# Row norm factors moved from GpSimd to VectorE, and a shorter inverse root, in a transformer block on one core

## The chip, the core and the metric

The kernel runs on one core of a Trainium2 chip. The core has TensorE (PE, matrix products), VectorE (DVE), ScalarE (ACT), GpSimd (POOL) and SyncE (SP, which issues most of the DMAs). The metric is the device time of one execution in microseconds, lower is better; the time given is the median of several runs.

## The reference

One block: two RMS norms with modulation, a mixer of four gated linear-attention heads (HGRN2) and four retention heads, run forwards and backwards over 2048 rows of width 1024, then a feed-forward part with a convolution of width 3 on its gate, and a final RMS norm. A context of 256 rows supplies the start states. What matters here are the norms: each row is multiplied with the inverse root of its mean square.

```python
def _rmsnorm(t, g):
    tf = t.astype(jnp.float32)
    y = tf * lax.rsqrt(jnp.mean(tf * tf, axis=-1, keepdims=True) + EPS)
    return (y * g.astype(jnp.float32)).astype(t.dtype)

hx = _rmsnorm(x, norm1_g[layer]) * (1.0 + sc1) + sh1
hc = _rmsnorm(ctx, norm1_g[layer]) * (1.0 + csc1) + csh1
...
hg_o = _rmsnorm(hg_o, hg_norm_g.reshape(HG_HEADS, 1, HG_DV))
ret_o = _rmsnorm(y_f + _flip(y_b), ret_norm_g.reshape(RET_HEADS, 1, RET_DV))
x = x + g1 * (mix_x.astype(x.dtype) @ w_out[layer])
hx2 = _rmsnorm(x, norm2_g[layer]) * (1.0 + sc2) + sh2
x = x + g2 * _conv_ffn(hx2, w_up[layer], conv_w[layer], conv_b[layer], w_down[layer])
return _rmsnorm(x, final_g)
```

## The kernel before, in words

The 2048 rows are four groups of 512; each group is four tiles of 128 rows on the partitions. Products in f16 are made of three passes each (`mm3`, L99 to L104: high times high, high times low, low times high), and the large matrices are multiplied in seven block products, whose sums and differences VectorE, ScalarE and, for the feed-forward weights, GpSimd form.

The program runs in this order. `setup` and `heads` (L1063) load the modulation weights and normalise group 3, the first one that is used. Then the eight heads are worked off in 32 steps, each with a group's sweep (the tiles K, Q, T and A, the products `sc`, `sf`, `kp`, `op`) woven together with the next step's projection (`hx` or `hc` times `w_z`, `w_q`, `w_vg`). Into the first of these steps the norms of the remaining rows are laid: group 2 and the context (called `gate` in the trace, after the tiles in which its rows lie) while the first projection runs, group 1 during step 0 and group 0 during step 1. After the heads come the output projection (`out_steps`, L1484), the feed-forward part and `ffn_down` (L1850), which ends with the final norm, row tile by row tile.

`norm_rows` (L395) does one group's norm: squares with row sums on ScalarE (and, for group 2, group 3 and the context, half of them on VectorE), their sum `ssq` on VectorE (L413), the inverse root by `rstd` (L414), and the scaling of the rows in place, half of each row on ScalarE (L419) and half on VectorE (L421). `first_blocks` (L431) then transposes the scaled rows on TensorE (`tp`, L428), applies the modulation on ScalarE (`ftmp`, L471) and forms the seven feature blocks `hx` (`hc` for the context).

There are two ways to the inverse root. `rstd` (L68) uses six operations on GpSimd: scale and add, a power of -0.5, and one Newton step. `rstd_v` (L80) uses twelve on VectorE: scale and add, a start value from the bits of the number in two operations, and three Newton steps of three operations. Both write the same small tiles `rs_v`, `rs_t` (one buffer) and `rs_y` (two buffers). `rstd` is called for the five norms in `norm_rows` and the 16 row tiles of `out_steps`; `rstd_v` for the 32 head norms (L997) and for the 16 row tiles of the final norm (L1912).

The order of the instructions on each engine is made by a scheduler from the program's dependences, its own estimates of durations, and hints in the code (`issue_after`, `high_priority`). Each engine then works its list off in order. So a few operations more or less on one engine change the places of many others.

Of the kernel before, what the change touches and what calls it, by code (L numbers as in the profile page):

```python
# [12 lines left out]
I32 = mybir.dt.int32  # L13
U8 = mybir.dt.uint8
AF = mybir.ActivationFunctionType
ALU = mybir.AluOpType
# [4 lines left out]
D = 1024  # L21
KT = D // P
G = 512
NG = SEQ // G
# [18 lines left out]
H = G // 2  # L43
RING = 10
SEQUENCE = 0, 1, 5, 6, 4, 3, 2

# [7 lines left out]
class Kern:  # L56
# [23 lines left out]
    def rstd_v(self, ssq, n, count):  # L80

        tt, ts, stt = self.nc.vector.tensor_tensor, self.nc.vector.tensor_scalar, self.nc.vector.scalar_tensor_tensor
        v, y, t = (self.wp.tile([P, 4], F32, tag=f"rs_{a}", bufs=1 + (a == "y"), name="rs_" + a)[:, :n] for a in "vyt")
        ts(v, ssq, 1.0 / count, EPS, ALU.mult, ALU.add)
        ts(t.bitcast(I32), v.bitcast(I32), 1, None, ALU.logical_shift_right)
        ts(y.bitcast(I32), t.bitcast(I32), -1, 0x5F3759DF, ALU.mult, ALU.add)
        for _ in range(3):
            stt(t, y, -0.5, y, ALU.mult, ALU.mult)
            tt(t, t, v, ALU.mult)
            stt(y, t, 1.5, y, ALU.add, ALU.mult)  # L90
        return y

    def ps(self, tag, shape, name):
# [301 lines left out]
    def norm_rows(self, g, xn, behind=None, both=False, late=None):  # L395

        nc = self.nc
        nt = len(xn)
        if g == NG - 1:
            self.junk = self.mp.tile([P, 512], F16, tag="qf3", bufs=1, name="junk")  # L400
        if both:
            junk = self.mp.tile([P, 512], F16, tag="Ta", bufs=1, name="junk")
        sq = self.mp.tile([P, 4, 2], F32, tag="sq8", bufs=2, name="sq8")
        for i in range(nt):
            for h in range(2):
                on_act = not both or h
                with self.tc.issue_after(behind[on_act].ins) if behind else nullcontext():
                    if on_act:
                        nc.scalar.activation(self.junk, xn[i][h], AF.Square, accum_out=sq[:, i, h:h + 1])
                    else:  # L410
                        nc.vector.scalar_tensor_tensor(junk, xn[i][h], 1.0, xn[i][h], ALU.mult, ALU.mult, accum_out=sq[:, i, h:h + 1])
        ssq = self.mp.tile([P, 4], F32, tag="ssq", bufs=2, name="ssq")
        nc.vector.tensor_tensor(ssq[:, :nt], sq[:, :nt, 0], sq[:, :nt, 1], ALU.add)  # L413
        r = self.rstd(self.mp, ssq[:, :nt], nt, D)  # L414
        for i in range(nt):
            for h in range(2):
                if h:
                    with self.tc.issue_after(late.ins) if late else nullcontext():
                        nc.scalar.activation(xn[i][h], xn[i][h], AF.Copy, scale=r[:, i:i + 1])  # L419
                else:  # L420
                    nc.vector.tensor_scalar(xn[i][h], xn[i][h], r[:, i:i + 1], None, ALU.mult)  # L421
        return xn
# [126 lines left out]

    def features(self, h, g, ms=SEQUENCE):  # L550

        if g in self.X:
            return self.X.pop(g)
        X = [None] * 7
        for m in ms:
            X[m] = self.slot_tile([P, 4, 2, H], F16, "hx", "hx")
            self.nc.sync.dma_start(X[m], self.hxd[g][m])
        return X
# [1473 lines left out]
```

## Time and profile before

| what | value |
|---|---|
| median of 3 runs | 2556.37 us (2556.28 to 2559.72) |
| the profiled execution | 2557.44 us, its span 2555.7 us |
| granted TensorE clock, mean | 0.990 |
| GpSimd busy | 386.9 us, nearly all of it in the feed-forward part |
| first and last GpSimd operation for `norm_rows` | 28.4 us, 147.9 us |
| operations of `rstd` and `rstd_v` | 21 calls on GpSimd, 48 calls on VectorE |

The page gives busy times by engine. Shares of the whole span say little here, since the kernel has stages with different limits; the busy times of stretches, and what each engine waited for in them, say more. A row of the timeline has start, duration, engine, line, operation, the tile written and those read, sizes and count, and in brackets the engine's idle time before it and what ended it.

### The profile page before, as it was taken

The numbers are of one execution on the slowest core, as the hardware profiler recorded it, in microseconds if no ns is written. First come the engines' busy times: TensorE is split into PE (matmuls) and PEld (weight loads), VectorE is DVE, ScalarE is ACT, GpSimd is POOL, SyncE is SP. The second block draws the span as 40 slices with busy tenths as digits, with TensorE's granted clock in tenths as the row PEclk, the third lists the DMA queues.
The fourth block names the chain that finished last, engine by engine and source line by source line (L and its number), as shares of the span: only waits on it lengthen the run. The fifth ranks groups of instructions, "written<-read, shape, count | busy, mean of one in ns | idle before, by whom it ended". The sixth has DMA issues, their size and how long they took to land.

```text
span 2555.7 us, 56261 instructions
## 1 busy us (share of the span) xinstructions
PE 2476.7 (97%) x22763; PEld 1644.6 (64%) x22763; DVE 1892.4 (74%) x4309; ACT 1354.8 (53%) x2886; POOL 386.9 (15%) x377
## 2 busy tenths in 40 slices
PE   6899999999999999999999999999999999999998
PEld 4688989898899999985454444444444444444443
DVE  6888787878677877875658888887888887224756
ACT  7786666656545544554556565555665555211221
POOL 1100000000000000001230343434343443000000
PEclk8899999999999999999999999999999999999999
DMA  8415243334466767785320233322333338534562
GB/s 313 169 63 193 90 159 131 115 124 142 162 207 211 265 213 247 254 313 194 106 78 30 85 114 120 108 107 99 110 113 104 108 130 301 205 142 157 216 221 78
DMA packets 144788, 402.36 MB, mean 157 GB/s; under 512 B 16143, under 2 KB 16371, under 8 KB 139920
## 3 DMA queue, kind: packets, MB, share of 16 engines
q1 hardware_dynamic: 134976, 381.81, 42.7%
q10 hardware_dynamic: 9248, 16.79, 2.0%
q8 instruction: 178, 2.92, 0.5%
q14 instruction: 82, 0.67, 0.1%
q0 software_dynamic: 304, 0.17, 0.0%
HBM read 302.77 MB, written 95.94 MB: 156 GB/s over the span
## 4 chain that ended last, share of the span: by engine, by line
PE 66%; DVE 16%; issue 6%; ACT 5%; DMA 5%; POOL 1%; SPq 0%; DVEq 0%; ACTq 0%; POOLq 0%
PE pa L102 7%; PE pa L103 7%; PE pa L104 7%; PE pd L104 5%; PE pd L102 5%; PE pd L103 5%; PE pc L102 3%; PE pc L104 3%; PE pc L103 3%; PE pb L102 2%; PE pb L103 2%; PE pb L104 2%; PE opp L103 2%; PE opp L104 2%; PE opp L102 2%
## 5 line engine op out<-in xcount | busy, mean ns | idle before, releaser
L104 PE MATMUL pa<-feat,w 128*128 128x512 f16 x704 | 266.6, 379 | 1.9 <-DVE w L704 1.9
L102 PE MATMUL pa<-feat,w 128*128 128x512 f16 x704 | 263.6, 379 | 4.6 <-ACT ta L596 4.5
L103 PE MATMUL pa<-feat,w 128*128 128x512 f16 x704 | 266.8, 379 | 0.0
L103 PE MATMUL pd<-wd,actl 128*128 128x512 f16 x616 | 233.3, 379 | 0.0
L104 PE MATMUL pd<-wd,actl 128*128 128x512 f16 x616 | 233.3, 379 | 0.0
L102 PE MATMUL pd<-wd,actl 128*128 128x512 f16 x616 | 232.6, 379 | 0.0
L104 PEld LDWEIGHTS <-w 128*128 128x128 f16 x1232 | 120.5, 98 | 147.5 <-DVE w L704 2.6
L103 PEld LDWEIGHTS <-w 128*128 128x128 f16 x1232 | 120.5, 98 | 144.9 <-issue 5.3
L102 PEld LDWEIGHTS <-w 128*128 128x128 f16 x1232 | 120.4, 98 | 142.1 <-ACT w L703 1.3
L103 PEld LDWEIGHTS <-hx 128*128 128x128 f16 x1824 | 179.4, 98 | 8.3 <-issue 6.4
L102 PEld LDWEIGHTS <-hx 128*128 128x128 f16 x1824 | 179.6, 99 | 1.8 <-ACT hx L447 0.2
L104 PEld LDWEIGHTS <-hx 128*128 128x128 f16 x1824 | 179.0, 98 | 1.4 <-DVE hx L448 0.7
L1507 POOL TENSOR_TENSOR ssq<-ssq 128x1 f32<-128x1 f32 x16 | 7.0, 439 | 1111.4 <-ACT junk L1502 1111.4
L1752 ACT ACTIVATE st<-act,modT 128x512 f16<-128x512 f32 x154 | 107.3, 717 | 114.8 <-DVE act L1742 64.9
L102 PE MATMUL pa<-w_vg,hx 128*128 128x128 f16 x896 | 160.6, 220 | 3.0 <-ACT ct L596 1.4
L104 PE MATMUL pa<-w_vg,hx 128*128 128x128 f16 x896 | 160.4, 220 | 0.5 <-DVE hx L448 0.5
L1753 DVE SCALAR_TENSOR_TENSOR st<-act,modT,st 128x512 f16<-128x512 f32 x154 | 142.6, 961 | 24.5 <-ACT st L1752 23.9
L103 PE MATMUL pa<-w_vg,hx 128*128 128x128 f16 x896 | 160.7, 220 | 0.0
L102 PE MATMUL pa<-hx,w_z 128*128 128x256 f16 x512 | 140.9, 275 | 6.4 <-ACT ct L596 4.1
L104 PE MATMUL pa<-hx,w_z 128*128 128x256 f16 x512 | 140.8, 275 | 1.9 <-issue 1.9
L103 PE MATMUL pa<-hx,w_z 128*128 128x256 f16 x512 | 140.9, 275 | 0.5 <-DVE hx L451 0.4
L102 PE MATMUL pc<-feat,w 128*128 128x512 f16 x352 | 133.4, 379 | 0.8 <-ACT w L703 0.8
(545 smaller groups left out, 7219.0 us busy)
## 6 DMA issues: line engine op xcount, KB each, us to landing
hx<-hxd SPq DMA_DIRECT2D x212, 512.0 KB, 5.0
actd<-st SPq DMA_DIRECT2D x154, 256.0 KB, 2.0
actl<-actd SPq DMA_DIRECT2D x28, 1024.0 KB, 5.2
wur<-in_w_up_dram SPq DMA_DIRECT2D x44, 512.0 KB, 3.6
raw<-in_w_in_dram SPq DMA_DIRECT2D x36, 512.0 KB, 4.7
wm<-in_w_mod_dram SPq DMA_DIRECT2D x64, 256.0 KB, 4.2
hxd<-hx SPq DMA_DIRECT2D x28, 512.0 KB, 3.6
wdb<-in_w_down_dram SPq DMA_DIRECT2D x44, 256.0 KB, 4.1
```

The lines of the kernel that those rows point to most:

```text
L102: mm(ps, lhs(0), rhs(0), start=start, stop=False, skip_group_check=True)
L103: mm(ps, lhs(0), rhs(1), start=False, stop=False, skip_group_check=True)
L104: mm(ps, lhs(1), rhs(0), start=False, stop=stop, skip_group_check=True)
L1507: nc.gpsimd.tensor_tensor(ssq[:, 0:1], ssq[:, 0:1], ssq[:, 1:2], ALU.add)
L1752: nc.scalar.activation(p[:, 0], v, AF.Copy, scale=s)
L1753: nc.vector.scalar_tensor_tensor(p[:, 1], v, s, p[:, 0], ALU.mult, ALU.subtract)
```

## The change

The row norm factors of every group but group 3 are made by `rstd_v` on VectorE in place of `rstd` on GpSimd; that is group 2, the context, group 1 and group 0. `rstd_v` itself gets nine operations in place of twelve: the start value comes from one operation in place of two, and three Newton steps are replaced by one polynomial of degree four in the deviation `v` of y*y*x from 1, which is evaluated in Horner's way and multiplied on. `rstd` on GpSimd stays for group 3 and for the 16 row tiles of `out_steps`.

```diff
+RSQ = 0.7235660666409525, -0.6910196001212606, 0.7162674493934401, -0.8287177420385489
...
         ts(v, ssq, 1.0 / count, EPS, ALU.mult, ALU.add)
-        ts(t.bitcast(I32), v.bitcast(I32), 1, None, ALU.logical_shift_right)
-        ts(y.bitcast(I32), t.bitcast(I32), -1, 0x5F3759DF, ALU.mult, ALU.add)
-        for _ in range(3):
-            stt(t, y, -0.5, y, ALU.mult, ALU.mult)
-            tt(t, t, v, ALU.mult)
-            stt(y, t, 1.5, y, ALU.add, ALU.mult)
+        ts(y.bitcast(I32), v.bitcast(I32), -0.5, float(0x5F3759DF), ALU.mult, ALU.add)
+        tt(t, y, y, ALU.mult)
+        tt(t, t, v, ALU.mult)
+        ts(v, t, RSQ[0], -RSQ[0], ALU.mult, ALU.add)
+        stt(t, v, RSQ[3], v, ALU.add, ALU.mult)
+        stt(t, t, RSQ[2], v, ALU.add, ALU.mult)
+        stt(t, t, RSQ[1], v, ALU.add, ALU.mult)
+        stt(y, t, 1.0, y, ALU.add, ALU.mult)
         return y
...
-        r = self.rstd(self.mp, ssq[:, :nt], nt, D)
+        r = self.rstd(self.mp, ssq[:, :nt], nt, D) if g == NG - 1 else self.rstd_v(ssq[:, :nt], nt, D)
```

Behind the changed function the line numbers are three higher than before (L421 becomes L424, L930 becomes L933).

The scheduler moves instructions over the first steps. On VectorE in step 0, around group 1's factor (`x` are group 1's rows, `T`, `cFG` and `ct`, `cb` tiles of the sweep and of projections), there stands before:

```order
L451 TENSOR_TENSOR hc_156<-ftmp,hc_156 128x2x128
L791 TENSOR_TENSOR T_1307<-FG 128x512
L421 TENSOR_SCALAR x_1201<-x_1201,rs_y 128x512
L421 TENSOR_SCALAR x_1203<-x_1203,rs_y 128x512
L421 TENSOR_SCALAR x_1205<-x_1205,rs_y 128x512
L421 TENSOR_SCALAR x_1207<-x_1207,rs_y 128x512
L791 TENSOR_TENSOR T_1772<-T_1307 128x256
L630 TENSOR_TENSOR ct<-pc,ct 128x128
L630 TENSOR_TENSOR cb<-pa,cb 128x128
```

and in the changed kernel:

```order
L87 TENSOR_TENSOR rs_t<-rs_y 128x4
L633 TENSOR_TENSOR ct<-pc,ct 128x128
L794 TENSOR_TENSOR T_1781<-T_1316 128x256
L88 TENSOR_TENSOR rs_t<-rs_t,rs_v 128x4
L633 TENSOR_TENSOR cb<-pa,cb 128x128
L89 TENSOR_SCALAR rs_v<-rs_t 128x4
L90 SCALAR_TENSOR_TENSOR rs_t<-rs_v 128x4
L91 SCALAR_TENSOR_TENSOR rs_t<-rs_t,rs_v 128x4
L788 TENSOR_SCALAR cFG<-cFG,omlb,lb 128x256
L92 SCALAR_TENSOR_TENSOR rs_t<-rs_t,rs_v 128x4
L93 SCALAR_TENSOR_TENSOR rs_y<-rs_t,rs_y 128x4
L424 TENSOR_SCALAR x_1207<-x_1207,rs_y 128x512
```

The T product and the two evacuations moved from behind the scaling to the midst of the chain of nine, whose first two operations stand further ahead.

On TensorE the transposes of group 1 (`tp`) stood right behind the context's last products with `w_z`:

```order
L103 MATMUL pa<-hc_157,w_z 128x128
L104 LDWEIGHTS w_z
L104 MATMUL pa<-hc_157,w_z 128x128
L428 MATMUL tp<-ident,x_1201 128x128
L428 MATMUL tp<-ident,x_1202 128x128
```

In the changed kernel 36 products stand between these two, the last of them products of `hx` (group 2's features) with `w_z`:

```order
L106 MATMUL pc<-hx,w_z 128x256
L107 LDWEIGHTS w_z
L107 MATMUL pc<-hx,w_z 128x256
L431 MATMUL tp<-ident,x_1207 128x128
L431 MATMUL tp<-ident,x_1208 128x128
```

Twelve of the 36 are products of the context, 128 columns wide, and 24 are of group 2, 256 wide; all of them stood behind the first twelve transposes before.

On VectorE in step 1, around group 0's factor (`x` are group 0's rows, K, Q and T the tiles of step 0's sweep), there stands before:

```order
L413 TENSOR_TENSOR ssq<-sq_2158 128x4
L791 TENSOR_TENSOR T_1930<-T_1891 128x32
L630 TENSOR_TENSOR ct<-pc,ct 128x256
L925 TENSOR_TENSOR K<-K,T_1891 128x2x16x16
L421 TENSOR_SCALAR x_2142<-x_2142,rs_y 128x512
L421 TENSOR_SCALAR x_2144<-x_2144,rs_y 128x512
L421 TENSOR_SCALAR x_2146<-x_2146,rs_y 128x512
L421 TENSOR_SCALAR x_2148<-x_2148,rs_y 128x512
L930 TENSOR_TENSOR Q<-Q,T_1891 128x2x16x16
```

and in the changed kernel, from the sixth operation of the chain on:

```order
L90 SCALAR_TENSOR_TENSOR rs_t<-rs_v 128x4
L928 TENSOR_TENSOR K<-K,T_1939 128x2x8x32
L933 TENSOR_TENSOR Q<-Q,T_1939 128x2x8x32
L91 SCALAR_TENSOR_TENSOR rs_t<-rs_t,rs_v 128x4
L794 TENSOR_TENSOR T_2275<-FG 128x512
L92 SCALAR_TENSOR_TENSOR rs_t<-rs_t,rs_v 128x4
L928 TENSOR_TENSOR K<-K,T_2275 128x2x128x2
L93 SCALAR_TENSOR_TENSOR rs_y<-rs_t,rs_y 128x4
L424 TENSOR_SCALAR x_2151<-x_2151,rs_y 128x512
L424 TENSOR_SCALAR x_2153<-x_2153,rs_y 128x512
L424 TENSOR_SCALAR x_2155<-x_2155,rs_y 128x512
L424 TENSOR_SCALAR x_2157<-x_2157,rs_y 128x512
```

The K and Q products of the sweep's sixth level (8x32), which the product `sf` of TensorE needs, stood behind the scaling and now stand in front of it; those of the fifth level (16x16) are now ahead of the sum `ssq`. On ScalarE, likewise, most of the copies of A (L940, and four of the six of L937) moved from behind its four scalings of group 0 to in front of them.

## What to expect of it

> **What bounds the kernel now.** I read the page's busy times first, then busy time by stage, then TensorE's waits inside the first 250 us, and last the end of the timeline.
>
> ```profile
> span 2555.7 us, 56261 instructions
> PE 2476.7 (97%) x22763; PEld 1644.6 (64%) x22763; DVE 1892.4 (74%) x4309; ACT 1354.8 (53%) x2886; POOL 386.9 (15%) x377
> 50.00:250.00 200.00, 181.93 (x2834) 161.43 (x2832) 177.03 (x425) 162.43 (x373) 11.92 (x24) 0.95 0.37 135
> 250.00:1200.00 950.00, 926.88 (x13163) 845.71 (x13163) 732.03 (x2014) 528.15 (x1321) 7.57 (x28) 1.00 0.56 187
> 1200.00:2400.00 1200.00, 1190.37 (x5910) 553.47 (x5909) 854.96 (x1489) 606.58 (x1082) 359.42 (x304) 1.00 0.37 128
> 2400.00:2546.40 146.40, 146.36 (x679) 66.13 (x676) 92.78 (x270) 22.01 (x53) 0.00 (x0) 1.00 0.46 165
> ```
>
> TensorE is the bound: it sits idle for 79 us of the span. From 250 us on it is idle for 23.1 us of 950, 9.6 of 1200 and nothing of the last 146, so a VectorE operation saved there is mostly saved beside TensorE. What the change can move is the stretch from 50 to 250 us, with 18.1 us of idle and a mean clock of 0.95, and the tail behind the last product.
>
> The four lines of TensorE's timeline that hold its longest waits near a norm factor, and the stretches of 2 us around them (columns: length, PE, PEld, DVE, ACT, POOL busy, then granted clock):
>
> ```profile
> 104.99 0.58 PE L428 MATMUL tp<-ident,x 128*128 128x128 f32 x3 [1.95 <-DVE x L421]
> 105.74 1.70 PE L428 MATMUL tp<-ident,x 128*128 128x128 f32 x9 [0.18 <-ACT x L419]
> 153.33 0.69 PE L918 MATMUL sf<-Q,K 128*64 128x64 f32 x16 [2.20 <-DVE Q L930]
> 154.85 0.80 PE L964 MATMUL op<-V,A 128*128 128x128 f32 x2 [0.83 <-ACT A L937]
> 106.00:108.00 2.00, 2.00 (x13) 1.36 (x12) 0.76 (x4) 2.00 (x5) 0.00 (x0) 0.67 0.00 0
> 108.00:110.00 2.00, 2.00 (x12) 1.44 (x11) 0.07 (x1) 1.89 (x4) 0.00 (x0) 0.50 0.00 0
> 154.00:156.00 2.00, 1.17 (x35) 0.93 (x38) 1.95 (x4) 0.82 (x4) 0.00 (x0) 0.61 0.00 0
> 156.00:158.00 2.00, 2.00 (x59) 1.94 (x48) 1.39 (x3) 1.53 (x3) 0.00 (x0) 0.50 0.04 8
> 158.00:160.00 2.00, 2.00 (x15) 1.94 (x14) 1.86 (x4) 1.98 (x7) 0.00 (x0) 0.50 0.02 4
> 160.00:162.00 2.00, 2.00 (x59) 1.90 (x59) 1.46 (x5) 2.00 (x6) 0.00 (x0) 0.68 0.00 0
> ```
>
> TensorE waits 2.13 us before group 1's transposes and 3.03 us while group 0's factor is made, and behind each wait it runs some microseconds at a lower clock. The work lost to that, (1 - clock) x busy: 0.66 + 1.00 = 1.7 us near 108, and 0.46 + 1.00 + 1.00 + 0.64 = 3.1 us near 158.
>
> Both waits begin at GpSimd:
>
> ```profile
> 98.76 0.15 DVE L413 TENSOR_TENSOR ssq<-sq 128x4 f32<-128x4 f32 x1
> 98.83 0.28 DVE L630 TENSOR_TENSOR ct<-pb,ct 128x128 f32<-128x128 f32 x1
> 99.00 3.12 POOL L72 TENSOR_SCALAR rs_v<-ssq 128x4 f32<-128x4 f32 x1 [28.55 <-DVE ssq L413]
> 104.12 0.20 POOL L77 TENSOR_TENSOR rs_y<-rs_y,rs_t 128x4 f32<-128x4 f32 x1
> 102.00:104.00 2.00, 1.03 (x19) 0.86 (x16) 0.06 (x1) 0.00 (x0) 1.67 (x5) 1.00 0.00 0
> 104.35 1.67 DVE L421 TENSOR_SCALAR x<-x,rs_y 128x512 f32<-128x512 f32 x4 [2.30 <-POOL rs_y L77]
> 104.35 2.56 ACT L419 ACTIVATE x<-x,rs_y 128x512 f32<-128x512 f32 x4 [2.59 <-POOL rs_y L77]
> 147.95 1.68 DVE L421 TENSOR_SCALAR x<-x,rs_y 128x512 f32<-128x512 f32 x4 [2.02 <-POOL rs_y L77]
> 147.95 2.56 ACT L419 ACTIVATE x<-x,rs_y 128x512 f32<-128x512 f32 x4 [2.77 <-POOL rs_y L77]
> 164.22 0.60 PE L428 MATMUL tp<-ident,x 128*128 128x128 f32 x4
> ```
>
> The factor comes 5.4 us after group 1's sum, and VectorE and ScalarE, which work in order, both stand still before it for 2.0 to 2.8 us. For group 0 nobody needs the scaled rows yet: their first transpose is at 164.22. The stall alone, sitting in front of the K and Q products, costs TensorE its 3.03 us.
>
> **The change, part by part.** Operations off the path first. 48 calls lose three operations each; dependent ones start 0.19 us apart:
>
> ```profile
> 2548.85 0.15 DVE L84 TENSOR_SCALAR rs_v<-cw 128x1 f32<-128x1 f32 x1
> 2550.97 0.16 DVE L90 SCALAR_TENSOR_TENSOR rs_y<-rs_t,rs_y 128x1 f32<-128x1 f32 x1
> 2551.16 1.42 DVE L1915 SCALAR_TENSOR_TENSOR c<-c,rs_y,fgb 128x512 f32<-128x512 f32 x2
> L89 DVE TENSOR_TENSOR rs_t<-rs_t,rs_v x144: 145/160/166, 261.1 to 2550.8; 128x4 f32<-128x4 f32 x96, 128x1 f32<-128x1 f32 x48
> ```
>
> *Tail.* The last call is on the path: 12 operations from 2548.85 to 2551.16, 0.193 each. Nine take 1.73 in place of 2.31: -0.6 us. The new operations are of the same forms and widths (145 to 166 ns), so I see no other price; were each 20 ns longer, 0.2 us would be given back. The 15 other calls of the last norm lie beside a TensorE that is never idle there: 0.
>
> *Head norms.* 32 calls x 3 x 0.19 = 18 us of VectorE time between 250 and 1200 us, where it is busy for 732 of 950. TensorE's idle of 23.1 us there is the most it could return; the other instructions change places too, which could cost as much as a lost load wait, so I bound it by -3 and +3 and take 0.
>
> *Group 1.* The VectorE chain stands between products and evacuations that used to wait behind the scaling. From the sum to the factor the new order holds what VectorE did without a pause from 98.76 to 102.06 (the row of 102 has it busy for 0.06 us), 3.3 us, some 0.8 us of evacuations and T from behind the scaling (an estimate from their widths, by the 0.28 of the evacuation at 98.83), and nine small operations, five of them at 0.07 (98.76 to 98.83: an independent follower starts that soon) and four at 0.19, 1.1 us. That is 5.2 us, about the 5.4 of before: the factor is not sooner. But VectorE does its work in the meantime, and TensorE has 36 products ahead of the transposes, 24 of them of the form below, which start 0.11 us apart: 2.6 us and more, for a wait of 2.13.
>
> ```profile
> 71.99 0.27 PE L102 MATMUL pb<-hx,w_q 128*128 128x256 f16 x1
> 72.10 0.27 PE L103 MATMUL pb<-hx,w_q 128*128 128x256 f16 x1
> ```
>
> So the wait goes and with it the low clock: -2.1 - 1.7 = -3.8; bounds 0 and -3.8.
>
> The Trainium skill, "TensorE: Matmul & The Clock Gate", section "What's actually happening", has the clock halve after an idle window of about 3.4 us. Here 2.13 us of idle in two pieces were followed by 0.50, so the rows speak for a lower limit; by the page's window the gap would not be the cause and the term would be -2.1.
>
> *Group 0.* K and Q products stand ahead of, or inside, the chain, and the four scalings behind. On VectorE's path to the product at 153.33 the stall of 2.02 and the scalings' 1.6 go, and six dependent and three single operations come, 6 x 0.19 + 3 x 0.07 = 1.4: 2.2 us sooner, just the wait of 2.20; besides, K by FG and the K and Q of one level more now stand ahead of the sum, not behind the factor. Most of ScalarE's copies of A move ahead of its scalings (2.77 + 2.46 us sooner), which covers the 0.83. The scaled rows come later but have 164.22 - 149.55 = 14.7 us to spare. So -3.0 - 3.1 = -6.1; bounds 0 and -6.1.
>
> *Group 2 and context.* Here the chain has a price.
>
> ```profile
> 64.92 0.16 DVE L413 TENSOR_TENSOR ssq<-sq 128x4 f32<-128x4 f32 x1
> 68.25 1.68 DVE L421 TENSOR_SCALAR x<-x,rs_y 128x512 f32<-128x512 f32 x4 [1.21 <-POOL rs_y L77]
> 68.44 0.22 PE L104 MATMUL pc<-w_vg,hx 128*128 128x128 f16 x1
> 70.98 0.86 DVE L421 TENSOR_SCALAR gate<-gate,rs_y 128x512 f32<-128x512 f32 x2
> 76.09 0.69 DVE L451 TENSOR_TENSOR hx<-ftmp,hx 128x512 f16<-128x512 f32 x1
> 80.00:90.00 10.00, 6.58 (x103) 4.16 (x102) 10.00 (x21) 10.00 (x25) 0.00 (x0) 0.98 0.86 316
> 90.00:100.00 10.00, 6.24 (x37) 4.55 (x37) 10.00 (x26) 8.96 (x27) 1.00 (x1) 0.51 0.50 203
> ```
>
> FG, cb and ct now stand inside the chain, and ct waits for a product that TensorE ends near 68.7. So group 2's factor comes near 69.6, 1.4 us late, but with FG, cb and ct done. The context's chain waits behind qs, K, Q and ks and ends near 75.8, against 70.98. Adding VectorE's rows up, it is about 0.6 us behind at 76 us, shortly before the stretch from 80 to 100 in which it has no idle time and ScalarE hardly any. I take +0.6; bounds -0.5 and the context's whole delay, +4.8.
>
> *VectorE's load.* The four groups bring 36 operations into a stretch where VectorE is busy for 177 of 200 us. Between independent work each costs 0.07, together +2.5; in a row, 0.19 each, +7.0. I take +2.5, since most stand between other work. It hides in VectorE's idle only if TensorE does not catch up with it, and it will: the terms of groups 1 and 0 take 10 us out of that stretch.
>
> *GpSimd and SyncE.* GpSimd loses 24 operations of 4 calls and nothing waits for it sooner. Some loads and stores of feature blocks and of raw weights change places on SyncE, which issues in order.
>
> ```profile
> ACT w_z L750 <- DMA raw<-in_w_in_dram: 26.8, 11, 4.3
> ```
>
> ScalarE's longest wait for such a load is 4.3 us, the most that one place further back should cost; the order moves some forward and some back, so I take 0, bounds -1 and +4.3.
>
> Sum: -0.6 + 0 - 3.8 - 6.1 + 0.6 + 2.5 = -7.4 us. The profiled execution took 2557.44 us (1.7 around its span), 1.1 above the median of 2556.37. So 2550.0 for it, and **2549.0** for the median.
>
> **Rivals.** (1) *VectorE becomes the bound.* The 36 operations cost 0.19 each and TensorE, come early, waits for K and Q products: -7.4 + (7.0 - 2.5) = -2.9, 2553.5. For it: VectorE is already full from 80 to 100. Against: 2.0 and 2.3 us of its own idle go at the same time. The skill's "VectorE: DVE Perf Modes", section "The DRAIN you can't avoid", holds that an operation starts only when the pipe has emptied, and advises fewer operations whatever their chaining; that is this rival. The pair at 98.76 and 98.83 speaks against it. (2) *Hidden anyway.* The factors come no sooner and something else is late: casts of feature blocks on ScalarE for group 1, sums of squares for group 0. Only the tail stays: 2555.8. (3) *Slower.* The context's factor is made behind FG, which waits for ScalarE's sigmoid, which now stands behind four scalings that wait for group 2's factor. If that circle costs the full 4.8 us at 76, all behind it is late by as much, TensorE's idle grows into a longer low clock (+3.1, as near 158), and groups 1 and 0 give nothing since VectorE is late when they come: +4.8 + 3.1 - 0.6 = +7.3, 2563.7. It decides once VectorE's first cast behind ks starts later than 78 us (76.1 now). (4) *Everything is returned:* no load, no delay: -10.5, 2545.9.
>
> **How the numbers follow.** Forecast 0.55, rival 1 0.15, rival 2 0.14, rival 3 0.08, rival 4 0.08. A measurement can tell 0.2%, 5.1 us: below 2551.3 is faster, above 2561.5 slower. Of the forecast's 0.55 I put 0.05 above 2551.3. Faster 0.50 + 0.08 = 0.58; same 0.05 + 0.15 + 0.14 = 0.34; slower 0.08. The range runs from 2543 (rival 4 and the head norms' -3) to 2558 (rival 2 with +2 from moved instructions).
>
> **What would show it.** Right: no wait of TensorE over 1 us before group 1's transposes and before sf and op of the first head, clock 1.00 there, nine operations of 1.7 us in the tail. Wrong at group 2: the first cast behind ks later than 77 us. Wrong at the load: new waits of TensorE on VectorE's K, Q or hx between 110 and 220 us. Wrong altogether: the tail is shorter and the first 250 us as long as before.

## The result, and the profile after

| | runs | median, us | lowest to highest |
|---|---|---|---|
| before | 6 | 2559.27 | 2556.28 to 2561.57 |
| after | 6 | 2542.45 | 2536.08 to 2547.92 |

The ratio of after to before is 0.9938, with a 95% interval of 0.9926 to 0.9949: the change makes the kernel faster by 0.6%, about 16 us. In the two profiled executions it is 14.8 us (spans 2555.7 and 2540.9). The forecast was -7.4 us, to 2549.0 us within 2543 to 2558: the direction came out, the gain is twice as large, and the median lies half a microsecond below the stated range. Two executions at a much lower clock are left out of all comparisons, one of 7359 us at 0.34 (the variant with one operation more behind the first head norm; of its trace only the order of the instructions is used) and one of 3199 us at 0.75 (the kernel before).

The page of the changed kernel begins as follows, and below it are two of the stretches shown for the kernel before (length, then PE, PEld, DVE, ACT and POOL busy, then the granted clock):

```profile
span 2540.9 us, 56141 instructions
PE 2469.5 (97%) x22763; PEld 1638.8 (64%) x22763; DVE 1880.3 (74%) x4201; ACT 1354.4 (53%) x2886; POOL 373.3 (15%) x353
50.00:250.00 200.00, 184.62 (x2927) 165.49 (x2926) 186.24 (x480) 166.14 (x386) 0.00 (x0) 0.97 0.39 142
250.00:1200.00 950.00, 929.92 (x13147) 843.91 (x13146) 722.10 (x1909) 534.65 (x1328) 10.36 (x35) 1.00 0.56 191
```

TensorE has the same number of products; its busy time falls by 7.3 us, since less of it is run at the low clock, and its idle time by 7.5 (14.8 less 7.3). In the first stretch the clock goes from 0.95 to 0.97 and the idle time from 18.1 to 15.4; in the second the idle time goes from 23.1 to 20.1.

Where along the program the gain arises is read from rows that both kernels have. The first `kp` of the third step (the first row before, the second after), and the end of the last norm, where nine operations are made in a row:

```profile
298.90 1.09 PE L947 MATMUL kp<-ident,K 128*128 128x128 f32 x8
```

```profile
291.01 1.09 PE L950 MATMUL kp<-ident,K 128*128 128x128 f32 x8
2534.64 0.15 DVE L85 TENSOR_SCALAR rs_v<-cw 128x1 f32<-128x1 f32 x1
2536.18 0.16 DVE L93 SCALAR_TENSOR_TENSOR rs_y<-rs_t,rs_y 128x1 f32<-128x1 f32 x1
2536.38 1.41 DVE L1918 SCALAR_TENSOR_TENSOR c<-c,rs_y,fgb 128x512 f32<-128x512 f32 x2
```

So 7.9 of the 14.8 us are there by 300 us. The chain of the tail takes 2536.38 - 2534.64 = 1.74 us in place of 2.31, 0.6 us. What is left, some 6 us, arises between 300 us and the end of the output projection, in the heads; a table further on divides it.

TensorE's waits from 50 to 110 us, and below them those from 110 to 170 us, in the changed kernel (sum, times, longest):

```profile
PE pb L105 <- DVE ct L633: 3.7, 1, 3.7
PE tp L431 <- ACT ftmp L474: 1.7, 4, 0.5
...
PE pa L105 <- ACT ct L599: 2.0, 2, 1.1
```

The wait of `tp` for `x` is gone, and so are those for Q and A. The longest one that is left was there before, 2.7 us long, and has grown by 1.0; two waits for `ct`, 2.0 us together, are new between 110 and 170 us. The stretches around the two places, and group 1's and group 2's rows:

```profile
102.00:104.00 2.00, 1.75 (x29) 1.63 (x29) 2.00 (x8) 1.05 (x4) 0.00 (x0) 1.00 0.00 0
106.00:108.00 2.00, 2.00 (x23) 1.88 (x21) 2.00 (x6) 2.00 (x4) 0.00 (x0) 1.00 0.00 0
150.00:160.00 10.00, 10.00 (x223) 9.62 (x222) 8.29 (x21) 9.42 (x20) 0.00 (x0) 1.00 0.02 4
100.18 0.16 DVE L416 TENSOR_TENSOR ssq<-sq 128x4 f32<-128x4 f32 x1
105.53 0.16 DVE L93 SCALAR_TENSOR_TENSOR rs_y<-rs_t,rs_y 128x4 f32<-128x4 f32 x1
107.34 1.36 PE L431 MATMUL tp<-ident,x 128*128 128x128 f32 x11
69.71 0.88 DVE L424 TENSOR_SCALAR x<-x,rs_y 128x512 f32<-128x512 f32 x2
75.84 0.89 DVE L424 TENSOR_SCALAR gate<-gate,rs_y 128x512 f32<-128x512 f32 x2
77.25 0.68 DVE L454 TENSOR_TENSOR hx<-ftmp,hx 128x512 f16<-128x512 f32 x1
```

The clock is full at both places. Group 1's factor is no quicker than before (105.53 + 0.16 - 100.18 = 5.5 us from the start of the sum; 104.12 + 0.20 - 98.76 = 5.6 before), and its first transposes start later (107.34, before 104.99), but TensorE has other products until then.

### The profile page after: what moved, and what is told of

Same layout as the page of the kernel before. It is cut to its first block, busy times and chain, and to the rows that moved or that the text cites. A ratio compares the mean times of both kernels' runs of the same rounds, so it can differ in the third digit from the quotient of the medians.

```text
span 2540.9 us, 56141 instructions
## 1 busy us (share of the span) xinstructions
PE 2469.5 (97%) x22763; PEld 1638.8 (64%) x22763; DVE 1880.3 (74%) x4201; ACT 1354.4 (53%) x2886; POOL 373.3 (15%) x353
## 4 chain that ended last, share of the span: by engine, by line
PE 74%; DVE 13%; ACT 5%; DMA 4%; issue 3%; POOL 0%; SPq 0%; DVEq 0%; ACTq 0%; POOLq 0%
PE pa L105 8%; PE pa L106 8%; PE pa L107 8%; PE pd L107 5%; PE pd L105 5%; PE pd L106 5%; PE pc L105 4%; PE pc L106 4%; PE pc L107 4%; PE pb L105 3%; PE pb L106 3%; PE pb L107 3%; PE opp L105 2%; PE opp L107 2%; PE opp L106 2%
```

## The experiments

Twelve variants ran. The one idea is that the move took away stalls of VectorE and with them TensorE's waits in the first 300 us; the others concern the 6 us in the heads: the time of the operations saved there, the scheduler's new order, or luck with the low clock. The table gives all results; "idle" is 600 us less TensorE's busy time from 720 to 1320 us of the profile, that is in the second half of the heads and the output projection, and "clock" is the granted clock, mean of all executions that are compared.

| variant | operations in a head norm | row factors on VectorE | median, us | ratio to before, 95% | idle, us | clock |
|---|---|---|---|---|---|---|
| before | 12 | none | 2556.8 to 2559.3 | 1 | 9.9 | 0.991 |
| the change | 9 | 2, context, 1, 0 | 2542.45 | 0.9938 (0.9926 to 0.9949) | 7.1 | 0.993 |
| move alone | 12 | the same, 12 operations | 2551.71 | 0.9979 (0.9967 to 0.9990) | 8.7 | 0.993 |
| polynomial alone | 9 | none | 2551.82 | 0.9973 (0.9960 to 0.9986) | 6.0 | 0.991 |
| change, heads with 12 | 12 | 2, context, 1, 0 | 2560.28 | 1.0001 (0.9993 to 1.0010) | 16.6 | 0.992 |
| tail alone | 12 | none | 2557.98 | 0.9996 (0.9987 to 1.0005) | 10.8 | 0.991 |
| heads with 10 | 10 | 2, context, 1, 0 | 2548.86 | 0.9974 (0.9965 to 0.9982) | 7.4 | 0.993 |
| heads with 11 | 11 | 2, context, 1, 0 | 2552.50 | 0.9987 (0.9976 to 0.9998) | 7.3 | 0.992 |
| heads with 15 | 15 | 2, context, 1, 0 | 2571.78 | 1.0056 (1.0038 to 1.0073) | 22.7 | 0.990 |
| one more behind the first | 9 (one: 10) | 2, context, 1, 0 | 2545.45 | 0.9952 (0.9937 to 0.9968) | - | 0.993 |
| one more behind the tenth | 9 (one: 10) | 2, context, 1, 0 | 2540.65 | 0.9942 (0.9930 to 0.9954) | 7.4 | 0.993 |
| group 0 alone | 9 | 0 | 2550.67 | 0.9974 (0.9964 to 0.9984) | 5.0 | 0.992 |
| group 1 alone | 9 | 1 | 2544.32 | 0.9942 (0.9926 to 0.9958) | 8.1 | 0.993 |
| all groups | 9 | 3, 2, context, 1, 0 | 2544.42 | 0.9950 (0.9935 to 0.9966) | 8.5 | 0.993 |

### Move and polynomial apart

Four kernels that combine the two parts of the change. The move alone keeps the old `rstd_v`; the polynomial alone keeps the old call:

```diff
-        r = self.rstd(self.mp, ssq[:, :nt], nt, D) if g == NG - 1 else self.rstd_v(ssq[:, :nt], nt, D)
+        r = self.rstd(self.mp, ssq[:, :nt], nt, D)
```

> Row factors of groups 2, 1, 0 and context on VectorE as in the change, but every inverse root keeps the twelve operations. Compared with the changed kernel's profile (14.8 us shorter than before: 7.9 up to 300 us, 6.3 between 300 and 1320 us, 0.6 in the tail). Theory A, two sources: the first 300 us give 7 to 8 by the move, and the heads' part needs the three operations less; then this kernel is 6 to 9 us shorter than before (three more operations in each of the four row chains give back up to 1.5), with the tail at 2.3 us. Rival B, all of it follows from the move: 13 to 15 us shorter. Rival C, all is the polynomial's: within 2 us of before.

> Nine operations in all 48 inverse roots on VectorE, row factors of all groups on GpSimd as before. Theory A: the waits of TensorE before group 1's transposes (2.1 us) and before sf and op of the first head (3.0 us) are as before, with the low clock; the heads give 2 to 6 us and the tail 0.6, so 3 to 7 us shorter than before. Rival B: only the tail, 0.6. Rival C: 13 to 15 us shorter.

In the other two, `rstd_n` is the old function with its twelve operations, called by the heads; "tail alone" keeps the old row factors too:

```diff
-        return self.rstd_v(ssq, 4, P)
+        return self.rstd_n(ssq, 4, P)
```

> The changed kernel with the twelve operations in the 32 head norms alone; row factors and the last norms keep the nine. Theory A: 7.9 + 0.6 = 8.5 us shorter than before (7 to 10), which is 4 to 8 longer than the changed kernel, the difference arising between 300 and 1320 us in TensorE's idle time there. Rival B: as the changed kernel, within 2 us. Rival C: within 2 us of before.

> Before with nine operations in the 16 calls of the last norm alone. All theories: the tail 1.7 us in place of 2.3, so 0.6 us shorter. Since nothing ahead of 2146 us differs in the program, anything beyond 0.6 measures the spread from one execution to another, low clock periods that do or do not fall on a gap among it.

The first `kp` of the third step shows the first 300 us by themselves. In this order: the move alone, the polynomial alone, the change with twelve in the heads, the tail alone.

```profile
292.06 1.09 PE L947 MATMUL kp<-ident,K 128*128 128x128 f32 x8
```

```profile
299.21 1.09 PE L950 MATMUL kp<-ident,K 128*128 128x128 f32 x8
```

```profile
289.82 1.09 PE L963 MATMUL kp<-ident,K 128*128 128x128 f32 x8
```

```profile
298.05 1.09 PE L963 MATMUL kp<-ident,K 128*128 128x128 f32 x8
```

With the move it stands at 289.8 to 292.1, without it at 298.1 to 299.2 (298.90 before). Part of these differences is older than the change: the executions are up to 2.6 us apart at the first transpose `tp` of a tile `x` (a row of group 3, at 44.26 us before). Counted from that transpose, as in the first column of the table under "How much for each operation", the move gives 8.1 us in the change, 7.3 with twelve in the heads, and 4.6 in the move alone, whose row factors have twelve operations each. Nine operations in place of twelve give nothing up to there.

For the whole time no theory held throughout. The polynomial alone came out where its first theory had it (3 to 7 us shorter than before), and the move alone close to its own (5.4 us by the ratio, 6 to 9 expected). But the change with twelve in the heads was expected 8.5 us shorter than before and is as long; the move alone, which has more operations than that kernel in the row factors and the tail and none less, is 5.6 us shorter (0.9979 against 1.0001, the intervals apart). An order that holds more work can be the shorter one. The polynomial alone gives 5.9 us beyond the tail (0.9973 against 0.9996).

What the slow one met is at the end of the heads. TensorE's row with the wait, the last head's norm ahead of it, and the store and load of the mixed rows (`mixd`, `mxf`), from its timeline:

```profile
1141.62 1.14 DVE L1380 SCALAR_TENSOR_TENSOR ou<-ou,rs_y,gate 128x128 f32<-128x128 f32 x4
1146.21 0.33 ACTq L1384 DMA_DIRECT2D mixd<-m  x1
1150.67 5.74 SPq L1487 DMA_DIRECT2D mxf<-mixd  x5
1154.08 0.72 ACT L1488 ACTIVATE mp<-mxf,smk 128x512 f16<-128x512 f32 x1 [5.10 <-DMA mxf<-mixd]
1154.86 0.61 PE L118 MATMUL opp<-wo,mp 128*128 128x512 f16 x1 [5.17 <-ACT mp L1488]
```

The rows that the output projection needs go from a head norm through memory and back, and in this order TensorE's next product is one that needs them: it waits 5.17 us. The move alone has the same twelve operations in the heads and no such wait in its trace.

### How much for each operation

Since order and load change together, the next kernels vary the load in steps, by multiplications with 1.0 behind the polynomial of the head norms, and two were meant to vary the order almost without load: one operation of 0.16 us more in the whole program.

```diff
         stt(y, t, 1.0, y, ALU.add, ALU.mult)
+        ts(y, y, 1.0, None, ALU.mult)
         return y
```

> The changed kernel with ten operations in the 32 head norms (one multiplication by 1.0 added to each). Twelve there cost 17.8 us more than nine (2560.3 against 2542.5). Theory A, VectorE's time in the heads is what counts: 17.8 / 3 = 5.9 us per operation added, so about 2548. Theory B, the scheduler's order counts, which the added operations change, and not their time: anywhere between 2542 and 2560, with the difference from the changed kernel in TensorE's idle and low clock after 300 us.

> As the run with ten, with eleven operations. Theory A: 2 x 5.9 us above the changed kernel, about 2554, and above the run with ten. Theory B: anywhere between 2542 and 2560, not necessarily above the run with ten.

```diff
-        return self.rstd_v(ssq, 4, P)
+        r = self.rstd_v(ssq, 4, P)
+        self.norms = getattr(self, "norms", 0) + 1
+        if self.norms == 1:
+            nc.vector.tensor_scalar(r, r, 1.0, None, ALU.mult)
+        return r
```

> The changed kernel with one operation of 0.16 us more in the whole program, a multiplication by 1.0 behind the first head norm; it changes the order of about a sixth of VectorE's instructions. Theory A: as the changed kernel, 2542.5 within 1.5 us. Theory B: off by 3 to 15 us, likely longer, the difference arising after 270 us.

> The same one operation behind the tenth head norm, so that the order differs from the changed kernel's only from about 480 us on. Theory A: 2542.5 within 1.5 us. Theory B: off by 2 to 15 us, the difference arising after 480 us.

Fifteen ran after these:

> The changed kernel with fifteen operations in the 32 head norms (six multiplications by 1.0 added to each). Medians so far: nine 2542.5, ten 2548.9, eleven 2552.5, twelve 2560.3. Theory A, VectorE's time in the heads counts in full: 5.9 us for each operation, 2578. Theory B, it counts in part, about half of 0.19 x 32 for each operation, the rest being the order's scatter: 2557 to 2568. Theory C, only the order: 2542 to 2560, no longer than with twelve.

Against before, nine, ten, eleven, twelve and fifteen operations give -15.9, -6.6, -3.3, +0.3 and +14.3 us (the ratio less 1, times 2557). The rise from nine to fifteen is 30.2 us for six operations, 5.0 each; with 0.19 us in 32 calls an operation is 6.1 us of VectorE's time. So on average about four fifths of it reach the end, where I had taken none. A single step of the row, 3 to 14 us, is not to be read; the row as a whole is.

The two variants with one operation more do not show what order is worth. They are 3.6 us (behind the first norm) and 1.0 us (behind the tenth) longer than the change, but the intervals overlap, and by tile names their traces hold the changed kernel's instructions in nearly the same order: all 4201 of VectorE's with the operation behind the first norm, all but 21 with the one behind the tenth, and not a sixth of them elsewhere, as I had expected. That order counts is seen only in the move alone against the change with twelve in the heads, above.

The traces say where the operations count. Each is divided here at three products of TensorE: the first `kp` of the third step, the first `rkp`, with which the sweeps of the retention heads begin, and the first product with `feat`, with which the feed-forward part begins. The last two, before, and the stretch between the first two, before and in the changed kernel:

```profile
722.02 0.61 PE L1231 MATMUL rkp<-ident,K 128*128 128x128 f32 x4
1323.68 0.38 PE L102 MATMUL pa<-feat,w 128*128 128x512 f16 x1
298.90:722.02 423.12, 410.35 (x6998) 379.83 (x6991) 329.82 (x904) 267.03 (x665) 0.00 (x0) 0.99 0.40 129
```

```profile
291.01:711.26 420.25, 407.50 (x6997) 377.68 (x6991) 324.45 (x871) 266.70 (x665) 0.00 (x0) 1.00 0.40 130
```

All profiled executions but the one at the low clock, in us; the first column counts from the first transpose `tp` of a tile `x`:

| variant | operations in a head norm | up to the third step | third step to `rkp` | `rkp` to `feat` |
|---|---|---|---|---|
| before | 12 | 254.6 | 423.1 | 601.7 |
| tail alone | 12 | 254.7 | 418.8 | 605.0 |
| move alone | 12 | 250.0 | 419.9 | 603.8 |
| change, heads with 12 | 12 | 247.3 | 422.1 | 613.4 |
| the change | 9 | 246.5 | 420.2 | 598.4 |
| polynomial alone | 9 | 255.9 | 422.6 | 599.4 |
| group 0 alone | 9 | 253.0 | 421.5 | 596.7 |
| group 1 alone | 9 | 247.3 | 422.9 | 599.9 |
| all groups | 9 | 247.2 | 420.9 | 602.8 |
| one more behind the tenth | 9 (one: 10) | 247.6 | 420.2 | 599.5 |
| heads with 10 | 10 | 247.8 | 426.4 | 601.7 |
| heads with 11 | 11 | 247.5 | 426.3 | 599.4 |
| heads with 15 | 15 | 246.3 | 422.3 | 621.7 |

The first column goes with the move: with group 1 on VectorE and nine operations it is 246.3 to 247.8, in eight kernels (seven of them in nearly the same order up to there); without it 253.0 to 255.9. The middle one holds 12 of the 32 head norms and shows no price for their operations: 420.2 to 422.9 with nine, 418.8 to 423.1 with twelve, 422.3 with fifteen. (Ten and eleven are 3 us above these.) The last one holds 19 of the norms, and there the price shows: 596.7 to 602.8 with nine, mean 599.4; 601.7 to 613.4 with twelve, mean 605.9; 621.7 with fifteen. Six more operations cost 22 us there and take 6 x 19 x 0.19 = 21.7 us of VectorE's time, the full price; three more cost 6.5 of 10.8; with ten and eleven (601.7 and 599.4) the scatter hides it. So the four fifths are a mean of nothing in one part and up to the full price in another. Each row is one execution: before and the tail alone are the same program in these columns and differ by 4.3 and 3.3 us in the last two, so such a difference between two rows is not to be read.

TensorE from 720 to 1320 us, first the change, then the heads with fifteen, and for the latter its three longest waits there:

```profile
720.00:1320.00 600.00, 592.94 (x5921) 478.96 (x5919) 441.39 (x1092) 303.77 (x723) 41.15 (x117) 1.00 0.63 217
```

```profile
720.00:1320.00 600.00, 577.34 (x5792) 471.70 (x5792) 449.11 (x1184) 296.85 (x707) 38.46 (x102) 0.99 0.63 215
PE opp L122 <- ACT mp L1492: 4.5, 2, 3.4
PE rob L1363 <- DVE Kt L1365: 4.4, 2, 3.4
PE rop L1356 <- DVE rA L1345: 3.1, 4, 1.4
```

The idle time is 22.7 us with fifteen and 7.1 with nine. VectorE is busy for only 441 to 449 of the 600, so it is not full; but TensorE waits some microseconds here and there for `Kt`, `rA` and the rows of `mp`. That these are late because VectorE's short chains stand ahead of them fits, but is not shown for any single wait. By the first table, six kernels with nine operations have 5.0 to 8.5 us of idle time in this stretch, mean 7.0, and four with twelve have 8.7 to 16.6, mean 11.5: 4.5 us for three operations. Ten and eleven do not differ from nine there.

### Group 1 and group 0 apart

```diff
-        r = self.rstd(self.mp, ssq[:, :nt], nt, D) if g == NG - 1 else self.rstd_v(ssq[:, :nt], nt, D)
+        r = self.rstd(self.mp, ssq[:, :nt], nt, D) if g != 0 else self.rstd_v(ssq[:, :nt], nt, D)
```

> The changed kernel with only group 0's row factor on VectorE; group 2, the context and group 1 on GpSimd. Read at the start of the third step's sweep (298.9 us before, 8 us sooner with all four moved). Theory A, the prediction's terms add up: group 1's wait of 2.1 us near 103 and the low clock behind it are as before, group 0's waits of 3.0 us and the low clock from 154.5 go, 5 to 6 us sooner at that mark. Rival: group 0's waits go only because all came earlier by the work on group 1; then less than 2 us. The median holds the nine operations of the heads as well (the kernel with the nine alone gained 5.7) and the scatter by order of up to 4 us: 2541 to 2551.

With `g != 1` in that line:

> Only group 1's row factor on VectorE. Theory A: the wait near 103 goes and the waits of 3.0 us ahead of the first head's sf and op stay, 3 to 4 us sooner at the third step's sweep. Rival: the low clock stays since it does not come from this wait, 2 us sooner. Median 2543 to 2553, with the same reservation.

The first transpose `tp` of a tile `x` and the first `kp` of the third step (298.90 before), before, with group 0 alone and with group 1 alone:

```profile
44.26 0.27 PE L428 MATMUL tp<-ident,x 128*128 128x128 f32 x1
```

```profile
42.04 0.27 PE L431 MATMUL tp<-ident,x 128*128 128x128 f32 x1
295.07 1.09 PE L950 MATMUL kp<-ident,K 128*128 128x128 f32 x8
```

```profile
41.91 0.27 PE L431 MATMUL tp<-ident,x 128*128 128x128 f32 x1
289.25 1.09 PE L950 MATMUL kp<-ident,K 128*128 128x128 f32 x8
```

Both executions were 2.2 to 2.4 us ahead at that transpose already, before anything differs that the move touches. Without that, group 0 alone gives 3.8 - 2.2 = 1.6 us and group 1 alone 9.7 - 2.4 = 7.3, nearly all that the four together give (8.1). The whole times agree: against the polynomial alone (0.9973), which has the same nine operations, group 0 alone gives nothing (0.9974) and group 1 alone 7.9 us (0.9942, the intervals apart). So the terms do not add as I had them. TensorE's waits from 110 to 170 us with group 0 alone:

```profile
PE sf L921 <- DVE Q L933: 1.6, 1, 1.6
PE sc L911 <- DVE Ad L936: 1.4, 1, 1.4
PE op L967 <- ACT A L940: 0.8, 1, 0.8
PE sc L911 <- DVE Q L933: 0.7, 1, 0.7
```

and with group 1 alone, followed by VectorE's and GpSimd's rows at group 0's factor, which GpSimd makes here as before:

```profile
PE pa L105 <- ACT ct L599: 1.0, 1, 1.0
138.48 0.17 DVE L794 TENSOR_TENSOR T<-T 128x16 f32<-128x16 f32 x1
139.00 0.20 POOL L73 TENSOR_SCALAR rs_v<-ssq 128x4 f32<-128x4 f32 x1 [70.89 <-DVE T L794]
141.62 0.20 POOL L78 TENSOR_TENSOR rs_y<-rs_y,rs_t 128x4 f32<-128x4 f32 x1
141.85 1.68 DVE L424 TENSOR_SCALAR x<-x,rs_y 128x512 f32<-128x512 f32 x4 [0.66 <-POOL rs_y L78]
```

Two rows of VectorE in the kernel before, to compare:

```profile
141.75 0.69 DVE L930 TENSOR_TENSOR Q<-Q,T 128x512 f32<-128x512 f32 x1 [1.56 <-PE sc L908]
150.34 0.17 DVE L791 TENSOR_TENSOR T<-T 128x16 f32<-128x16 f32 x1
```

With group 1 on VectorE the waits for Q and A are gone although group 0's factor still comes from GpSimd: GpSimd starts on it at 139.00 in place of 144.95, and VectorE stalls for 0.66 us in place of 2.02. Turned round, group 0's move without group 1's leaves 4.5 us of waits there, more than the 3.0 before.

That VectorE was merely late since group 1's stall does not fit: before, it stood idle for 1.56 us until 141.75, waiting for TensorE. What the rows do show is another order. The T product of 16 columns stands ahead of group 0's scaling with group 1 alone (138.48, the scaling at 141.85), and the next K and Q products follow it there; before it stood behind the scaling (150.34 and 147.95). So the scheduler's order around group 0 changed with group 1's move. The runs do not say how much of the gain is the missing stall and how much the order that goes with it.

### All groups

```diff
+        r = self.rstd_v(ssq[:, :nt], nt, D)
```

> The changed kernel with group 3's factor on VectorE too, so that no row norm ahead of the output projection uses GpSimd. GpSimd's six operations there take 3.2 us (28.4 to 31.6) in the chain that ends last. If VectorE's nine at 0.19 replace them, 1.3 us sooner ahead of the first projection; if VectorE's weight preparation behind them is what counts, nothing. In the whole 2536 to 2546, since the order changes as well.

Its ratio is 0.9950, the interval overlapping that of the change; so no gain from group 3 is seen, and no variant here is clearly better than the change.

## Why the prediction was right, and where it was not

- **Tail**, -0.6: as forecast, 1.74 us for nine. By itself it is too small to be measured (tail alone, 0.9996).
- **Group 2 and context**, +0.6: two places came out as worked out by adding up rows: the scaling of group 2 starts at 69.71 (near 69.6 forecast), that of the context at 75.84 (75.8). But the first cast behind `ks` starts at 77.25, 1.2 us later than before and not 0.6, and so behind the 77 that was to show the prediction wrong at group 2. The execution was 0.3 us behind from its start, so the term is about 0.9; the wait for `ct` that grew by 1.0 may be its price. The 78 from which the slower rival would have decided was not reached, and that rival is out.
- **Group 1**, -3.8: wait and low clock went, as forecast, with a factor that comes no sooner. But the term stops too early: with group 1 alone 7.3 us are gained up to the third step.
- **Group 0**, -6.1: the waits went, but not because of this factor; alone it gives 1.6 and leaves them. The step that failed is "the stall alone, sitting in front of the K and Q products, costs TensorE its 3.03 us". I had put a wait down to the last stall ahead of it, where the kernel with group 1 alone loses the wait and keeps GpSimd in that place. That the four terms up to the third step together came near the forecast (-6.8, measured -8.1) is in part luck: group 1's was too small and group 0's too large.
- **VectorE's load**, +2.5: the sum up to 300 us, terms of group 1, group 0, group 2 and load, was -6.8, and it was -7.9 (-8.1 counted from the first transpose). I can't separate this term; no new wait for K or Q is seen up to 220 us, and rival 1 (VectorE becomes the bound there, 2553.5) is out.
- **Head norms**, 0 with bounds of -3 and +3: mis-sized, and this is why the size was off by half. The runs show 4 to 7 us for the three operations: 6.5 in the traces (605.9 less 599.4 from `rkp` to `feat`; 4.0 without the 613.4 and its wait of 5.17 us), 5.9 in the whole times (the polynomial alone against the tail alone). With the factors on VectorE it is 10 to 16 (the change against the two kernels with the move and twelve operations, 0.9979 and 1.0001), order included. The reason given, that operations are saved beside a busy TensorE, holds for the gated heads, where their number shows nothing. It fails in the retention heads and the output projection, where TensorE waits for products of VectorE and ScalarE, and where the operations added for fifteen cost their full time.
- **The profiled pair**: of the some 6 us in the heads, 3.3 arise from `rkp` to `feat` (601.7 less 598.4; 2.8 of it idle time, 9.9 less 7.1) and belong to that term. The other 2.9 arise from the third step to `rkp`, and not through saved operations: TensorE is idle for the same 12.8 us there in both (423.12 - 410.35 and 420.25 - 407.50), but before it ran two periods of 3.41 us at half the clock, from 331.95 and 673.28, and in the changed kernel none, 3.4 us of work. The tail alone, the same program up to there, met none in its execution and took 418.8. So this part is luck; the last section shows how such periods come and go.

By the traces, 8 us up to the third step, 6.5 from `rkp` to `feat` and 0.6 in the tail make some 15 us, as measured.

Over the executions, not the profiled ones alone, the mean span is 14.9 us shorter (2555.5 and 2540.6), and the mean clock rises from 0.9906 to 0.9933. That is 2550 x 0.0027 = 6.9 us less lost to the low clock, counted over the whole span, and some 8 us less idle time.

The Trainium skill, "VectorE: DVE Perf Modes", section "Rules for kernel authors", advises for chained operations to keep their number small. The runs agree for the part from `rkp` to `feat`, where dependent operations 0.19 us apart cost up to their full time although VectorE is a quarter idle; for the gated heads no run shows that it pays.

## What to carry to other kernels

A wait of the bounding engine need not be due to the last stall ahead of it in its supplier's list; a kernel that takes away one stall alone shows whose it is. Operations on an engine that is a quarter idle are not free everywhere: here they cost nothing in one part of the heads and up to their full time in another, so vary their number over a wide range and read the traces part by part before costing them at nothing. Where a scheduler makes the order, a kernel with more work can be the shorter one by 5.6 us of 2550, so read a smaller step only from several kernels. And take out first what two executions differ by before the change can act, here up to 2.6 us at 44 us.

## What the hardware showed besides

In the clock records of the 13 traces that are compared, all periods of half clock, but for the last of each, which the end cuts off, are multiples of 3.41 us long, and in one execution they start on one grid of 3.413 us whose phase differs from execution to execution. The Trainium skill, "TensorE: Matmul & The Clock Gate", section "What's actually happening", gives such a free-running window of 3413 ns; the traces agree. It has the clock fall after an idle window. Here a window need not be idle throughout, as the rows of the prediction already spoke for: in the kernel before, the window ahead of each of the five periods between 60 and 2500 us held 1.9 to 2.6 us of idle time; two other windows with 1.9 were not followed by a period, so around there both occur. In the 13 traces together, between 60 and 2500 us, of the windows at full clock with under 1.0 us of idle time none of 8985 was followed by half clock, with 1.0 to 1.6 us 3 of 116, with 1.6 to 2.0 us 26 of 57, and with 2.0 us or more all 32. (The ends of matmuls are modelled, so the true edge may be sharper.) So the same gap halves the clock or not by where it falls. This is the kernel before, the end of a gap and the clock behind it, and then the changed kernel at the same product:

```profile
331.63 0.27 PE L102 MATMUL pa<-hx,w_z 128*128 128x256 f16 x1 [2.24 <-ACT ct L596]
332.00:334.00 2.00, 2.00 (x12) 1.44 (x10) 0.72 (x2) 1.25 (x3) 0.00 (x0) 0.50 0.90 354
```

```profile
323.73 0.27 PE L105 MATMUL pa<-hx,w_z 128*128 128x256 f16 x1 [2.23 <-ACT ct L599]
324.00:326.00 2.00, 2.00 (x20) 1.71 (x18) 0.62 (x2) 1.62 (x5) 0.00 (x0) 1.00 0.94 383
```

By the grid all 2.24 us of the first gap lie in one window, while the second has 1.93 in one and the rest in the one before it. A gap of this size thus costs 1.7 us more in some executions, half of one period. That can be part of the scatter of 12 us among runs of the changed kernel: the shortest (2536.08) had a mean clock of 0.995, the longest (2547.92) 0.993. And a wait that is cut below that size can save more than its own length.
